# Bias tiles of one head loaded two heads ahead, value products one score group later, and a larger early part of the output projection, in a hybrid attention layer on one Trainium2 core

## The chip, the core and the metric

The kernel runs on one core of one Trainium2 chip. A core has five engines that work through queues of their own: TensorE (PE, matrix products), VectorE (DVE), ScalarE (ACT), GpSimd (POOL) and SyncE (SP), which here issues every DMA. They meet only at semaphores. The metric is the device time of one execution in microseconds (us); lower is better.

## What is computed

One layer of a hybrid decoder, for one sequence of 512 tokens and width 1024, with 256 memory tokens. The part that the change touches is the first block:

```python
h = rms_norm(x, norm_mix[l])
proj = h @ w_in[l]
qa, ka, va, qg, kg, vg, glr, rg = jnp.split(proj, offsets, axis=-1)
o_a = moba_attention(qa, ka, va, rp_table)      # 8 heads of 64, causal, with a bias by distance
o_g = gla_chunked(qg, kg, vg, log_a)            # 4 heads of gated linear attention
o_g = rms_norm(o_g, g_norm[l]).reshape(B, T, G_WIDTH) * jax.nn.silu(rg)
x = x + jnp.concatenate([o_a, o_g], axis=-1) @ w_out[l]
h = rms_norm(x, norm_xattn[l])
...
```

Cross attention into the memory tokens, a squared-ReLU MLP of width 4096 and a final norm follow; their code is the same before and after. With 512 tokens and blocks of 256 every past block is chosen, so the attention is plain causal attention with a bias that depends on the distance of query and key alone.

## The kernel before

**Numbers.** Each operand of a product is split into two fp16 parts, so one product of a 128-wide piece of the contraction is three matmuls (lines 227, 228, 229). One such piece, three matmuls, is called a step here. A generator yields after each step.

**Order.** The order on PE is written out by hand: `fill` is a queue of generators, and `fill(n)` takes n steps from it, between the pieces of the attention. The order on DVE, ACT, POOL and SP comes from a scheduler, and each of these works strictly through its own queue. The contraction of the output projection has eight pieces, `mix[0]` to `mix[7]`: `mix[p]` for p below 4 is the attention output of head pair p, and `mix[4]` to `mix[7]` are the gated linear attention heads, multiplied with their gate by `rg_steps`.

**Bias.** `bscr` in DRAM holds a bias table for each head. `Pair(p)` loads 128x256 of it for each of its two heads into one tile `bq` (two such tiles exist) and lets POOL spread column 256 over the left half.

**Attention.** The eight heads are taken as four pairs. For pair i and for g = 0 to 3, `score(3 - g)` makes the scores of 128 queries, of 512, 384, 256 and 128 keys, in two PSUM banks `s`. DVE adds the bias and takes the maximum (`p`, line 748), ACT takes the exponential (line 752), and after every second group the sums are inverted and ACT and DVE write the two fp16 parts of the probabilities (`pq`, lines 772 and 773). `trans()` sends the two heads' `pq` through two DMA transposes into `pT` (line 779). `attn_out(p)` multiplies `pT` with the values in 24 matmuls into a bank `o` (line 791), and ACT and DVE split it into `mix[p]` (lines 273 and 274). It is issued in the loop of the next pair, at g = 2. Between the groups `fill` brings the projections of pairs 2 and 3 (`qk`), then the four gates (`rg`).

**Output projection.** It is made in eight parts of 128 columns. For the first four, `early_steps` fills four PSUM banks with the pieces of `mix` that are there first, for all 512 tokens; `residual_steps` adds the rest, for each half of 256 tokens, adds the sum to `xr` (line 831) and collects squares for the norm. `ssq[hf].total()` sums them on PE, and `normed` makes `act2` of them, on which the next projection `xq` starts.

**Weights.** DMA brings them into five tiles `wst` of 512 KB; ACT and DVE turn each into two fp16 parts in one of ten tiles `whl` (lines 114 and 115). These conversions stand in the same queues.

Of the kernel before, what the change touches and what calls it, by code (L numbers as in the profile page):

```python
# [10 lines left out]
F32 = mybir.dt.float32  # L11
I32 = mybir.dt.int32
AF = mybir.ActivationFunctionType
ALU = mybir.AluOpType
AX = mybir.AxisListType

P = 128
T = 512
# [3 lines left out]
NEG = -1e30  # L22
# [16 lines left out]
def hybrid_block_kernel(  # L39
# [3 lines left out]
    nc = tc.nc  # L43
    PE, ACT, DVE, POOL = nc.tensor, nc.scalar, nc.vector, nc.gpsimd
# [16 lines left out]
    def gbank(name):  # L61
        return bank("pg", 3, name)

    def sbank(name):
        return bank("ps", 5, name)
# [155 lines left out]
    def gemm_steps(ps, key, act, c0=0, c1=T, kts=range(8), start=True, stop=True, base=0, **kw):  # L221
        wt = W.get(key).rearrange("p s (k c) -> p s k c", k=8)
        kts = list(kts)
        for i, kt in enumerate(kts):
            a = act[base + kt]
            st, sp = start and i == 0, stop and i == len(kts) - 1
            PE.matmul(ps, wt[:, 0, kt, :], a[:, 0, c0:c1], start=st, stop=False, **kw)  # L227
            PE.matmul(ps, wt[:, 0, kt, :], a[:, 1, c0:c1], start=False, stop=False, **kw)  # L228
            PE.matmul(ps, wt[:, 1, kt, :], a[:, 0, c0:c1], start=False, stop=sp, **kw)  # L229
            yield  # L230
# [39 lines left out]
    fill = Fill()  # L270
# [79 lines left out]
    mix = [m.bitcast(F16).rearrange("p (s t) -> p s t", s=2) for m in mixf]  # L350
    s1 = ExitStack()
    p1 = s1.enter_context(tc.tile_pool(name="p1", bufs=1))
# [46 lines left out]
    for n in range(8):  # L399
        ps = (sbank if n < 2 else gbank)(f"xk{n}")[:, :M]  # L400
# [28 lines left out]
    for c in range(2):  # L429
        for t in range(2):  # L430
            ps = gbank(f"xv{c}{t}")
# [21 lines left out]
    for i in range(2):  # L453
        for a, b in ((0, 0), (0, 1), (1, 0)):
            for j in range(4):
                kt = 2 * j + i
                PE.matmul(psg[32 * j:32 * j + 16, :], wg[:, a, kt, :], act1[kt][:, b, :],
                          start=(i == 0 and a == 0 and b == 0), stop=(i == 1 and a == 1),
# [220 lines left out]
    bscr = pdr.tile([8, P, T], F32, name="bscr")  # L679
# [3 lines left out]
        bass.AP(tensor=bscr1.tensor, offset=bscr1.offset, ap=[[NDIST, 8], [0, P], [1, NDIST]]),  # L683
    )

    gl = [Gla(0), Gla(1)]
    fill.add(gqk_steps(1), *[vg_steps(t) for t in range(4)])
    fill.add(*[va_steps(t) for t in range(4)], qk_steps(0), qk_steps(1))
    for pr in range(2):
        G = gl[pr]  # L690
        a = G.prep_fine()
        fill(20 if pr == 0 else 4)
        G.banks()
        G.small(0, a)
        for i, s in enumerate((8, 16)):
            a = G.prep_level(s)
            fill(2)
            G.small(128 + 128 * i, a)
        a = G.prep_level(32)
        fill(4)  # L700
        G.mid(a[0])
        a = G.prep_level(64)
        fill(4)
        G.large(a[0])
        G.prep_cross()
        fill(5)
        G.keys()
        fill(5)
        if pr == 0:
            fill.until(6)  # L710
        G.states()
        fill(4)
        G.outp()
        fill(6)
        for hh in range(2):
            G.norm(hh)
            fill(4)
# [5 lines left out]
    pt = s3.enter_context(tc.tile_pool(name="patt", bufs=1, reuse_waits="tile"))  # L723
# [3 lines left out]
    class Pair:  # L727
        def __init__(self, p):
            self.p, self.pr = p, {}
            bq = self.bq = pt.tile([P, 2, T], F32, tag="bq", bufs=2, name=f"bq{p}")  # L730
            for hh in range(2):
                nc.sync.dma_start(bq[:, hh, 256:], bscr[2 * p + hh, :, 127:383])
                POOL.tensor_copy(bq[:, hh, :256], bq[:, hh, 256:257].to_broadcast([P, 256]))
            self.sm = pt.tile([P, 3, 4, 2], F32, tag="sm4", bufs=2, name=f"sm4_{p}")

        def score(self, qt):
            p = self.p
            n = P * (qt + 1)
            pss = [sbank(f"s{p}_{qt}_{hh}")[:, :n] for hh in range(2)]
            qs = slice(qt * P, qt * P + P)  # L740
            for i, (a, b) in enumerate(((0, 0), (0, 1), (1, 0))):
                for hh, ps in enumerate(pss):
                    r = slice(64 * hh, 64 * hh + 64)
                    PE.matmul(ps, aq[p][r, a, qs], ak[p][r, b, :n], start=i == 0, stop=i == 2)
            mx, ng, sm = (self.sm[:, i, qt, :] for i in range(3))
            for hh, ps in enumerate(pss):
                s = self.pr[qt, hh] = pt.tile([P, n], F32, tag=f"p{qt}", bufs=2, name=f"p{p}_{qt}_{hh}")
                DVE.tensor_tensor_reduce(s, ps, self.bq[:, hh, T - n:], scale=1.0, scalar=NEG, op0=ALU.add, op1=ALU.max, accum_out=mx[:, hh:hh + 1])
            DVE.tensor_scalar(ng, mx, -1.0 / (SA * SA), None, op0=ALU.mult)
            for hh in range(2):  # L750
                s = self.pr[qt, hh]
                ACT.activation(s, s, AF.Exp, bias=ng[:, hh:hh + 1], scale=1.0 / (SA * SA), accum_out=sm[:, hh:hh + 1])
            if qt % 2 == 0:
                r = self.sm[:, 2, qt:qt + 2, :]
                DVE.reciprocal(r, r)
                DVE.tensor_scalar(r, r, SP, None, op0=ALU.mult)
                for q in (qt + 1, qt):
                    self.parts(q)
# [55 lines left out]
    early = {}  # L814

    def early_steps():
        for n in range(NPRE):
            early[n] = sbank(f"out{n}")
            yield from gemm_steps(early[n], ("out", n), mix, 0, T, (0, 1, 4, 5), stop=False, skip_group_check=True)

    def residual_steps(nm, act, hf, ssq):
        c0 = hf * HT
        for n in range(8):
            if nm == "out" and n < NPRE:
                ps = early[n][:, c0:c0 + HT]
                yield from gemm_steps(ps, (nm, n), act, c0, c0 + HT, (6, 7, 2, 3), start=False, skip_group_check=True)
            else:
                ps = gbank(f"{nm}{n}_{hf}")[:, :HT]
                yield from gemm_steps(ps, (nm, n), act, c0, c0 + HT)
            xs = xr[n][:, c0:c0 + HT]  # L830
            DVE.scalar_tensor_tensor(xs, ps, IS, xs, op0=ALU.mult, op1=ALU.add)
            ssq.add(xs)
# [8 lines left out]
    HT = T // 2  # L841
# [3 lines left out]
    for i in range(5):  # L845
        if i < 4:
            pairs[i] = Pair(i)
        if i in (2, 3):
            fill.until({2: 5, 3: 4}[i])
        if i == 4:  # L850
            fill.drain()
            load_xr()
            fill.add(early_steps(), residual_steps("out", mix, 0, ssq[0]))
        for g in range(4):
            if i < 4:
                pairs[i].score(3 - g)
                fill(2)
            if g > 0 and i >= 1:
                fill(2 if i < 4 else 4)
            if 1 <= i < 4 and g == 2:  # L860
                attn_out(pairs.pop(i - 1))
        if i < 4:
            pairs[i].trans()
            fill(2)
    fill(3)
    attn_out(pairs.pop(3))
    fill(1)
    s3.close()
    s1.close()

# [385 lines left out]
    for i, (a, b) in enumerate(parts[1:]):  # L1256
        ps = sbank(f"c3{i}")[:, :b - a]
# [100 lines left out]
```

## Time and profile before

| what | value |
|---|---|
| median of 3 runs | 724.23 us (721.04 to 724.78) |
| the profiled execution, its own time | 722.87 us |
| its span from first to last instruction | 721.1 us |
| PE busy | 686.4 us, 95% of the span |
| DVE busy | 551.3 us, 76% |
| ACT busy | 417.8 us, 58% |
| mean granted PE clock, as a share of full speed | 0.977 |

All times inside the execution are counted from the start of the span. A PE that is 95% busy leaves some 35 us in which it did nothing; where such a stretch lies, and whether what follows ran at full clock, is to be read from the timeline, stage by stage, since a mean over the span mixes stages with different limits.

### The profile page before, as it was taken

How to read it: one execution, taken by the hardware profiler on the slowest of the kernel's cores; microseconds unless marked ns; L12 is line 12 of the kernel's file. 1: busy time of each engine (PE TensorE's matmuls, PEld its weight loads, DVE VectorE, ACT ScalarE, POOL GpSimd, SP SyncE). 2: the span in 40 equal slices, each digit the busy share in tenths (PEclk: the TensorE clock that was granted, in tenths of full speed). 3: DMA queues.
4: the chain of work that ended last, by engine and by line, in shares of the span. 5: the costliest groups of instructions: out<-in, count | busy, mean ns of one | idle time of the engine just before them, and what ended most of it. 6: DMA issues, size and time to landing. Idle time of an engine off the chain costs nothing.

```text
span 721.1 us, 13438 instructions
## 1 busy us (share of the span) xinstructions
PE 686.4 (95%) x5370; PEld 472.7 (66%) x5370; DVE 551.3 (76%) x971; ACT 417.8 (58%) x803; POOL 81.7 (11%) x97
## 2 busy tenths in 40 slices
PE   6998999997889989999999999999999999999995
PEld 3843455453334478788888864458888866478884
DVE  7799772748858936947638899989887889999725
ACT  6686543545858816546536676565444766665633
POOL 4601000000000024200024200000000000003211
PEclk7999999999879999999999999999999999999998
DMA  8665722008366633316412423213333342314003
GB/s 315 225 237 183 257 88 89 2 30 262 71 153 147 202 101 118 117 41 165 129 20 77 157 78 99 72 46 119 117 117 117 119 149 86 116 39 143 26 1 118
DMA packets 56627, 85.62 MB, mean 119 GB/s; under 512 B 32075, under 2 KB 37492, under 8 KB 56564
## 3 DMA queue, kind: packets, MB, share of 16 engines
q1 hardware_dynamic: 56564, 84.76, 37.8%
q8 instruction: 42, 0.69, 0.4%
q14 instruction: 21, 0.17, 0.1%
HBM read 75.30 MB, written 3.68 MB: 110 GB/s over the span
## 4 chain that ended last, share of the span: by engine, by line
PE 55%; DVE 9%; ACT 3%; issue 2%; POOL 1%; DMA 1%; DVEq 0%; ACTq 0%; POOLq 0%
PE up L229 6%; PE up L227 6%; PE up L228 6%; PE a L1132 4%; PE a L1134 4%; PE a L1133 4%; DVE whl L115 2%; PE xq L229 2%; PE xq L228 2%; PE xq L227 2%; PE c L1132 2%; PE c L1133 2%; PE c L1134 2%; PE xo L229 1%; PE xo L228 1%
## 5 line engine op out<-in xcount | busy, mean ns | idle before, releaser
L115 DVE SCALAR_TENSOR_TENSOR whl<-wst,whl 128x1024 f16<-128x1024 f32 (+1 forms) x162 | 196.2, 1218 | 30.4 <-ACT whl L114 29.9
L114 ACT ACTIVATE whl<-wst 128x1024 f16<-128x1024 f32 (+1 forms) x162 | 165.6, 1029 | 32.4 <-PE a L1134 8.0
L229 PEld LDWEIGHTS <-whl 128*128 128x128 f16 x784 | 77.4, 99 | 48.3 <-issue 5.2
L227 PEld LDWEIGHTS <-whl 128*128 128x128 f16 x784 | 77.3, 99 | 46.1 <-issue 7.0
L228 PEld LDWEIGHTS <-whl 128*128 128x128 f16 x784 | 77.4, 99 | 39.3 <-issue 1.5
L227 PE MATMUL up<-act,whl 128*128 128x512 f16 (+1 forms) x224 | 78.1, 349 | 0.0
L228 PE MATMUL up<-act,whl 128*128 128x512 f16 (+1 forms) x224 | 78.1, 349 | 0.0
L229 PE MATMUL up<-act,whl 128*128 128x512 f16 (+1 forms) x224 | 78.1, 349 | 0.0
L1132 PE MATMUL a<-t,whl 128*128 128x256 f16 x192 | 52.3, 273 | 1.1 <-ACT v L1149 1.1
L1134 PE MATMUL a<-t,whl 128*128 128x256 f16 x192 | 52.3, 273 | 0.0
L1133 PE MATMUL a<-t,whl 128*128 128x256 f16 x192 | 52.3, 273 | 0.0
L1133 PEld LDWEIGHTS <-whl 128*128 128x128 f16 x456 | 44.6, 98 | 6.9 <-issue 1.5
L1132 PEld LDWEIGHTS <-whl 128*128 128x128 f16 x456 | 44.6, 98 | 5.2
L1134 PEld LDWEIGHTS <-whl 128*128 128x128 f16 x456 | 44.6, 98 | 5.0
L228 PE MATMUL xq<-act,whl 128*128 128x256 f16 x128 | 34.9, 273 | 0.2 <-DVE act L274 0.2
L229 PE MATMUL xo<-ox,whl 128*128 128x256 f16 x128 | 34.9, 273 | 0.0
L227 PE MATMUL xq<-act,whl 128*128 128x256 f16 x128 | 34.9, 273 | 0.0
L227 PE MATMUL xo<-ox,whl 128*128 128x256 f16 x128 | 34.9, 273 | 0.0
L228 PE MATMUL xo<-ox,whl 128*128 128x256 f16 x128 | 34.9, 273 | 0.0
L229 PE MATMUL xq<-act,whl 128*128 128x256 f16 x128 | 34.9, 273 | 0.0
L273 ACT ACTIVATE t<-hs 128x512 f16<-128x512 f32 x32 | 19.8, 624 | 23.9 <-DVE hs L1014 23.7
L227 PE MATMUL out<-mix,whl 128*128 128x256 f16 (+1 forms) x112 | 32.2, 288 | 0.0
(335 smaller groups left out, 1661.0 us busy)
## 6 DMA issues: line engine op xcount, KB each, us to landing
wst<-in_w_up SPq DMA_DIRECT2D x32, 512.0 KB, 3.7
wst<-in_w_down SPq DMA_DIRECT2D x32, 512.0 KB, 4.3
wst<-in_w_tt SPq DMA_DIRECT2D x16, 512.0 KB, 4.5
wst<-in_w_xv SPq DMA_DIRECT2D x8, 512.0 KB, 4.7
wst<-in_w_vv SPq DMA_DIRECT2D x8, 512.0 KB, 4.2
wst<-in_w_out SPq DMA_DIRECT2D x8, 512.0 KB, 4.7
wst<-in_w_xq SPq DMA_DIRECT2D x8, 512.0 KB, 3.8
wst<-in_w_xo SPq DMA_DIRECT2D x8, 512.0 KB, 4.4
```

Of the source, the lines that this page charges most:

```text
L114: ACT.activation(wt[:, 0, c], stg[:, c], AF.Copy, scale=SW)
L115: DVE.scalar_tensor_tensor(wt[:, 1, c], stg[:, c], SW, wt[:, 0, c], op0=ALU.mult, op1=ALU.subtract)
L227: PE.matmul(ps, wt[:, 0, kt, :], a[:, 0, c0:c1], start=st, stop=False, **kw)
L228: PE.matmul(ps, wt[:, 0, kt, :], a[:, 1, c0:c1], start=False, stop=False, **kw)
L229: PE.matmul(ps, wt[:, 1, kt, :], a[:, 0, c0:c1], start=False, stop=sp, **kw)
L273: ACT.activation(dst_h, src, AF.Copy, scale=scale)
L1132: PE.matmul(ps, w[:, 0, kt, :], b[:, 0, c], start=st, stop=False, skip_group_check=not start)
L1133: PE.matmul(ps, w[:, 0, kt, :], b[:, 1, c], start=False, stop=False, skip_group_check=not start)
L1134: PE.matmul(ps, w[:, 1, kt, :], b[:, 0, c], start=False, stop=sp, skip_group_check=not start)
```

## The change

Three edits. The bias tiles become tiles of one head. Four slots exist, three in a pool that is open throughout (`p1`), one in the attention's pool (`pt`), and `load_bias(p)` is called once before the second half of the gated linear attention, for pair 0, and then at the start of each pair for the next one. `attn_out(i - 1)` moves from g = 2 to g = 3, behind one more score group and its fill steps. And `early_steps` takes six of the eight pieces in place of four, in 24 steps instead of 16, all of them ahead of `attn_out(3)`.

```diff
+    bias = {}
+
+    def load_bias(p):
+        bias[p] = []
+        for hh in range(2):
+            h = 2 * p + hh
+            if h % 4 < 3:
+                bq = p1.tile([P, T], F32, tag="bq", bufs=3, name=f"bq{h}")
+            else:
+                bq = pt.tile([P, T], F32, tag="bq", bufs=1, name=f"bq{h}")
+            nc.sync.dma_start(bq[:, 256:], bscr[h, :, 127:383])
+            POOL.tensor_copy(bq[:, :256], bq[:, 256:257].to_broadcast([P, 256]))
+            bias[p].append(bq)
...
     for pr in range(2):
+        if pr == 1:
+            load_bias(0)
...
     class Pair:
         def __init__(self, p):
             self.p, self.pr = p, {}
-            bq = self.bq = pt.tile([P, 2, T], F32, tag="bq", bufs=2, name=f"bq{p}")
-            for hh in range(2):
-                nc.sync.dma_start(bq[:, hh, 256:], bscr[2 * p + hh, :, 127:383])
-                POOL.tensor_copy(bq[:, hh, :256], bq[:, hh, 256:257].to_broadcast([P, 256]))
+            self.bq = bias.pop(p)
...
-            yield from gemm_steps(early[n], ("out", n), mix, 0, T, (0, 1, 4, 5), stop=False, skip_group_check=True)
+            yield from gemm_steps(early[n], ("out", n), mix, 0, T, (0, 1, 4, 5, 6, 7), stop=False, skip_group_check=True)
...
-                yield from gemm_steps(ps, (nm, n), act, c0, c0 + HT, (6, 7, 2, 3), start=False, skip_group_check=True)
+                yield from gemm_steps(ps, (nm, n), act, c0, c0 + HT, (2, 3), start=False, skip_group_check=True)
...
             pairs[i] = Pair(i)
+            if i < 3:
+                load_bias(i + 1)
...
-            if 1 <= i < 4 and g == 2:
+            if 1 <= i < 4 and g == 3:
                 attn_out(pairs.pop(i - 1))
...
-    fill(3)
+    fill(12)
     attn_out(pairs.pop(3))
-    fill(1)
```

On SP, at the start of the attention, the bias loads of before stood behind six loads of output weights (`wst44` to `wst46` are the last of them; `bq0` and `bq1` are pairs here, `pT0` are pair 0's transposes).

```order
L113 DMA wst44_2613<-in_w_out 128x1024
L113 DMA wst45_2631<-in_w_out 128x1024
L113 DMA wst46_2649<-in_w_out 128x1024
L732 DMA bq0_1831<-bscr_832 128x256 x2
L732 DMA bq1_1972<-bscr_832 128x256 x2
L113 DMA wst47_2667<-in_w_out 128x1024
L732 DMA bq2_2161<-bscr_832 128x256 x2
L779 DMA_TRANSPOSE pT0_0_1953<-pq0_0_1881 128x20x128
L779 DMA_TRANSPOSE pT0_1_1955<-pq0_1_1882 128x20x128
```

In the changed kernel (`bq` is numbered by head) the first three loads stand in the gated linear attention, ahead of the last five loads of `w_tt`, and the fourth to sixth take the old place.

```order
L113 DMA wst35_1788<-in_w_tt 128x1024
L697 DMA bq0_1393<-bscr_832 128x256
L697 DMA bq1_1396<-bscr_832 128x256
L697 DMA bq2_1838<-bscr_832 128x256
L113 DMA wst36_1860<-in_w_tt 128x1024
...
L113 DMA wst46_2665<-in_w_out 128x1024
L697 DMA bq3_1841<-bscr_832 128x256
L697 DMA bq4_1980<-bscr_832 128x256
L697 DMA bq5_1983<-bscr_832 128x256
L113 DMA wst47_2689<-in_w_out 128x1024
L793 DMA_TRANSPOSE pT0_0_1960<-pq0_0_1888 128x20x128
L793 DMA_TRANSPOSE pT0_1_1962<-pq0_1_1889 128x20x128
```

The loads of heads 0, 1 and 2 moved far ahead; those of heads 4 and 5 now stand ahead of pair 0's transposes and reuse the slots of heads 0 and 1.

On PE, in the first of the four early banks (`out0` is the bank, `mix5` the second gated head), the next bank followed after `mix5`:

```order
L227 MATMUL out0_2612<-mix5_110,whl41_2349 128x512
L228 LDWEIGHTS whl41_2349
L228 MATMUL out0_2612<-mix5_110,whl41_2349 128x512
L229 LDWEIGHTS whl41_2349
L229 MATMUL out0_2612<-mix5_110,whl41_2349 128x512
L227 LDWEIGHTS whl42_2458
L227 MATMUL out1_2630<-mix0_105,whl42_2458 128x512
L228 LDWEIGHTS whl42_2458
```

Now `mix6` and `mix7` follow in the same bank, and every other early step stands behind them:

```order
L229 MATMUL out0_2616<-mix5_110,whl41_2358 128x512
L227 LDWEIGHTS whl41_2358
L227 MATMUL out0_2616<-mix6_111,whl41_2358 128x512
L228 LDWEIGHTS whl41_2358
L228 MATMUL out0_2616<-mix6_111,whl41_2358 128x512
L229 LDWEIGHTS whl41_2358
L229 MATMUL out0_2616<-mix6_111,whl41_2358 128x512
L227 LDWEIGHTS whl41_2358
L227 MATMUL out0_2616<-mix7_112,whl41_2358 128x512
```

So the first use of `mix6` is the fifth of now 24 early steps, and the first use of `mix7` the sixth; before, 15 of the 16 early steps stood ahead of `attn_out(3)`, and none of the 16 used `mix6` or `mix7`.

On DVE, the end of the attention before (`pq3` are the last probabilities of pair 3, `rge`, `rgu` and `rg` tiles of the gates of heads 2 and 3, which end in `mix6` and `mix7`):

```order
L773 SCALAR_TENSOR_TENSOR pq3_0_2403<-p3_0_0_2509,sm4_3_2364,pq3_0_2403 128x128
L773 SCALAR_TENSOR_TENSOR pq3_1_2404<-p3_0_1_2511,sm4_3_2364,pq3_1_2404 128x128
L809 SCALAR_TENSOR_TENSOR rge2_2542<-rg2_2456,rgu2_2543 128x512
L803 TENSOR_SCALAR rge3_2584<-rge3_2584 128x512
L810 TENSOR_TENSOR rge2_2542<-rge2_2542,mix6_111 128x512
L115 SCALAR_TENSOR_TENSOR whl50_2860<-wst50_2859,whl50_2860 128x1024
L274 SCALAR_TENSOR_TENSOR mix6_111<-rge2_2542,mix6_111 128x512
L807 SCALAR_TENSOR_TENSOR rge3_2584<-rge3_2584,rgu3_2585 128x512
L808 SCALAR_TENSOR_TENSOR rgu3_2585<-rge3_2584,rgu3_2585 128x512
L809 SCALAR_TENSOR_TENSOR rge3_2584<-rg3_2554,rgu3_2585 128x512
L810 TENSOR_TENSOR rge3_2584<-rge3_2584,mix7_112 128x512
L274 SCALAR_TENSOR_TENSOR mix7_112<-rge3_2584,mix7_112 128x512
```

The same in the changed kernel; the last write of `pq3` stands four rows ahead of the first row shown:

```order
L115 SCALAR_TENSOR_TENSOR whl49_2830<-wst49_2829,whl49_2830 128x1024
L822 SCALAR_TENSOR_TENSOR rgu2_2547<-rge2_2546,rgu2_2547 128x512
L817 TENSOR_SCALAR rge3_2588<-rge3_2588 128x512
L823 SCALAR_TENSOR_TENSOR rge2_2546<-rg2_2460,rgu2_2547 128x512
L115 SCALAR_TENSOR_TENSOR whl50_2864<-wst50_2863,whl50_2864 128x1024
L824 TENSOR_TENSOR rge2_2546<-rge2_2546,mix6_111 128x512
L821 SCALAR_TENSOR_TENSOR rge3_2588<-rge3_2588,rgu3_2589 128x512
L822 SCALAR_TENSOR_TENSOR rgu3_2589<-rge3_2588,rgu3_2589 128x512
L274 SCALAR_TENSOR_TENSOR mix6_111<-rge2_2546,mix6_111 128x512
L823 SCALAR_TENSOR_TENSOR rge3_2588<-rg3_2558,rgu3_2589 128x512
L824 TENSOR_TENSOR rge3_2588<-rge3_2588,mix7_112 128x512
L274 SCALAR_TENSOR_TENSOR mix7_112<-rge3_2588,mix7_112 128x512
```

Ten rows stood between the last write of `pq3` and `mix7`; now it is 15: `mix5`, `mix2`, the rest of gate 2, two weight conversions and gate 3 come behind `pq3`.

## Rows read from the trace of the kernel before

**Rows 1.** The page, busy time by engine: us, share of the span, instructions.

```profile
PE 686.4 (95%) x5370; PEld 472.7 (66%) x5370; DVE 551.3 (76%) x971; ACT 417.8 (58%) x803; POOL 81.7 (11%) x97
```

**Rows 2.** Waits of PE, 160 to 300 us: total us, times, longest.

```profile
PE o L791 <- DMA pT<-pq: 8.6, 4, 3.3
```

**Rows 3.** Windows: busy us of PE, weight loads, DVE, ACT, POOL; PE clock, DMA.

```profile
140.00:160.00 20.00, 20.00 (x191) 11.09 (x188) 10.31 (x25) 8.39 (x20) 0.00 (x0) 1.00 0.01 2
...
179.60:183.00 3.40, 3.40 (x15) 1.06 (x16) 2.34 (x12) 2.25 (x7) 0.29 (x1) 0.52 0.03 12
...
201.30:206.70 5.40, 5.40 (x34) 3.15 (x34) 1.28 (x6) 0.88 (x2) 0.00 (x0) 0.50 0.31 125
254.40:256.60 2.20, 0.09 (x3) 0.02 (x2) 0.69 (x1) 0.41 (x1) 0.00 (x0) 1.00 1.03 192
...
226.95:255.53 28.58, 27.44 (x152) 12.30 (x150) 26.76 (x63) 21.15 (x46) 0.00 (x0) 1.00 0.82 199
...
276.97:293.50 16.53, 16.42 (x149) 14.48 (x148) 15.99 (x30) 13.60 (x26) 8.44 (x7) 1.00 0.38 128
```

**Rows 4.** Timeline of DVE: start, us, instruction, [idle before it and its releaser].

```profile
172.43 0.75 DVE L662 SCALAR_TENSOR_TENSOR mix<-go,gneg,wg 128x512 f32<-128x512 f32 x1
...
176.08 0.75 DVE L662 SCALAR_TENSOR_TENSOR mix<-go,gneg,wg 128x512 f32<-128x512 f32 x1
178.84 0.69 DVE L748 CUSTOM_DVE_ANT_0 p<-s,bq 128x512 f32<-128x512 f32 x1 [2.02 <-POOL bq L733]
```

**Rows 5.** Timeline of PE, 176 to 205 us.

```profile
176.88 0.28 PE L744 MATMUL s<-qks,qks 64*128 64x256 f16 x1 [1.40 <-DVE mix L662]
179.59 0.70 PE L744 MATMUL s<-qks,qks 64*128 64x256 f16 x5 [2.43 <-DVE sm L748]
...
191.84 0.39 PE L227 MATMUL qk<-act,whl 128*128 128x512 f16 x1
...
194.23 0.38 PE L229 MATMUL qk<-act,whl 128*128 128x512 f16 x1
197.35 0.63 PE L791 MATMUL o<-pT,vas 128*64 128x512 f16 x1 [2.74 <-DMA pT<-pq]
201.25 3.36 PE L791 MATMUL o<-pT,vas 128*64 128x512 f16 x23 [3.27 <-DMA pT<-pq]
```

**Rows 6.** SP's first transposes, all transposes' time to landing, and the bias copies.

```profile
192.16 6.34 SPq L779 DMA_TRANSPOSE pT<-pq  x2
...
DMA to landing us min/median/max: 4.9/5.1/6.5
...
L733 POOL COPY bq<-bq x8: 396/426/653, 178.4 to 209.4; 128x256 f32<-128x256 f32 x8
```

**Rows 7.** Timeline of DVE: the last probabilities of each pair, and mix7.

```profile
190.96 1.40 DVE L773 SCALAR_TENSOR_TENSOR pq<-p,sm,pq 128x256 f16<-128x256 f32 x4
...
208.35 1.68 DVE L773 SCALAR_TENSOR_TENSOR pq<-p,sm,pq 128x256 f16<-128x256 f32 x4 [0.64 <-ACT pq L772]
...
225.15 1.41 DVE L773 SCALAR_TENSOR_TENSOR pq<-p,sm,pq 128x256 f16<-128x256 f32 x4 [0.64 <-ACT pq L772]
...
247.09 1.00 DVE L773 SCALAR_TENSOR_TENSOR pq<-p,sm,pq 128x256 f16<-128x256 f32 x3
...
254.84 0.69 DVE L274 SCALAR_TENSOR_TENSOR mix<-rge,mix 128x512 f16<-128x512 f32 x1 [0.69 <-ACT mix L273]
```

**Rows 8.** Timeline of PE and DVE: the last value products, and their split.

```profile
256.57 1.79 PE L791 MATMUL o<-pT,vas 128*64 128x512 f16 x23 [2.11 <-DMA pT<-pq]
...
259.03 0.69 DVE L274 SCALAR_TENSOR_TENSOR mix<-o,mix 128x512 f16<-128x512 f32 x1 [3.50 <-ACT mix L273]
```

**Rows 9.** Timeline of PE and DVE: the norm behind the output projection.

```profile
276.97 0.60 PE L327 MATMUL ssqout<-accout,ones 128*128 128x256 f32 x2
...
293.10 0.41 DVE L274 SCALAR_TENSOR_TENSOR act<-ynout,act 128x256 f16<-128x256 f32 x1
...
296.95 0.70 PE L327 MATMUL ssqout<-accout,ones 128*128 128x256 f32 x2 [1.37 <-POOL accout L322]
```

More of the change, by code (lines that the diff above doesn't have):

```diff
@@ L747, in score @@
                 s = self.pr[qt, hh] = pt.tile([P, n], F32, tag=f"p{qt}", bufs=2, name=f"p{p}_{qt}_{hh}")
-                DVE.tensor_tensor_reduce(s, ps, self.bq[:, hh, T - n:], scale=1.0, scalar=NEG, op0=ALU.add, op1=ALU.max, accum_out=mx[:, hh:hh + 1])
+                DVE.tensor_tensor_reduce(s, ps, self.bq[hh][:, T - n:], scale=1.0, scalar=NEG, op0=ALU.add, op1=ALU.max, accum_out=mx[:, hh:hh + 1])
             DVE.tensor_scalar(ng, mx, -1.0 / (SA * SA), None, op0=ALU.mult)
```

## Prediction

> **What bounds the kernel now.** I read the page first: PE is busy for 686.4 of the 721.1 us of the span [rows 1], so it is the bound nearly everywhere, and a change of order can gain only where PE stands still. The sum of PE's waits in the stretch that the change touches names the largest: 8.6 us in four waits of the value products for the DMA transposes [rows 2]. The timeline then shows the places. PE stops before the scores of 256 keys of pair 0, 1.40 and then 2.43 us [rows 5]; the second wait ends when DVE has read the first scores, and DVE itself had stood still for 2.02 us until POOL had spread the bias [rows 4]. At `attn_out(0)` PE waits 2.74 and 3.27 us for the two transposes [rows 5], and at `attn_out(3)` 2.11 us [rows 8]. The windows show what follows a wait: after the first place the granted clock is 0.52 for 3.4 us, after the second 0.50 for 5.4 us, which is the 1.2 GHz level; around the 2.11 us it stays at 1.00 [rows 3]. The second thing to see is DVE. From the first maximum of pair 3 to `mix7` it is busy for 26.76 of 28.58 us [rows 3]: the end of the attention is DVE's, not PE's.
>
> **The change, step by step.** I follow the new queues with the durations of before. A step is 12 matmuls in four, so from 191.84 to 194.23 with 11 spacings 0.217 us a matmul, 0.65 us a step [rows 5].
>
> *Bias.* The loads of heads 0 to 2 now go out some 75 us before they are read, so the wait of DVE for POOL goes. What is late next is DVE's own queue: from 172.43 to 176.08 [rows 4] it runs five instructions (a `mix`, a weight conversion, three short ones), the new order has the same five ahead of the first maximum, and that starts at 176.1 instead of 178.84. The second `mix`, which frees a score bank, now stands behind it and ends near 177.4; PE then goes on at 177.4 instead of 179.6, after a wait of about 2.1 us, and I take no fall of clock there (the 2.11 us wait had none, the 2.43 us wait did). The copies on POOL are as many as before; three of them, at most 0.65 us each [rows 6], move to about 136 us, where they could hold DVE for 0 to 2 us, but PE is never idle there, 20.00 of 20 us busy [rows 3], so I take 0. The six bias loads ahead of pair 0's transposes on SP end when pair 0's scores are read, at about 180.4, long before the transposes can start; 0 to 0.5 us, and I take 0.
>
> *Pair 0 to the transposes.* DVE ended pair 0's probabilities at 190.96 + 1.33 = 192.3, 13.4 us after the first maximum [rows 4, 7]. The new order puts one `mix` (0.65) and one conversion (1.14) in between, and takes away waits for scores of about 2.2; I get 13.0 us, the end at 189.1.
>
> *Value products one group later.* Between the old and the new place of `attn_out(0)` lie one score group (0.3) and four steps (2.6). From 177.4 PE has 20 steps (13.0) and six score groups (2.9) to go and arrives at 193.3. The second transpose landed at 201.25, 9.1 us after the first was issued [rows 5, 6]; 189.1 + 9.1 = 198.2. So the wait doesn't go: it is 4.9 us in place of 6.0, because pair 0 moved PE forward too. After such a wait the clock was at 0.50 [rows 3], so the products take 3.36 us again (1.79 at full clock, as the last ones do [rows 5, 8]; bounds 0 and 1.6 us for the fall): the end is 201.5 instead of 204.6.
>
> *The chain to mix7.* ACT stands behind these products in its queue, so pair 1 can't pass them: a split, a conversion and the last probabilities need 4.1 us, the end of pair 1 is 205.6 (before 208.35 + 1.66 = 210.0 [rows 7]). Pair 2 took 16.5 us from there to 226.5, with 3.5 us of waits of DVE; its scores are now long ready and I take 2.1 us off: 220.0. From there to `mix7` it was 29.0 us, to 255.5 [rows 7]. DVE is the limit, and its new queue holds one conversion (1.14) less: 28.1 us. So `mix7` is there at 248.1 and, 2.6 us of queue earlier, `mix6` at 245.5. That is 7.4 us earlier than before.
>
> *More early steps.* From 201.5 PE has 44 steps to the first use of `mix6` (28.6), eight score groups (4.1), two products (4.4) and 0.6 of low clock: it arrives at 239.2. There is nothing else it could issue, since 19 steps stand behind in its queue. **A new wait** of 6.3 us for `mix6`, one step, 1.9 us for `mix7`. Then two matmuls and 18 steps (12.1), the last products without a wait (2.2), and the price of the clock: between 0 and 2.8 us (what 5.4 us at half clock cost, less its floor: 1.57 in the products and 1.2 in the steps [rows 3, 5]); I take the middle, 1.4. End of the last products: 248.1 + 12.1 + 2.2 + 1.4 = 263.8, against 256.57 + 1.79 = 258.4 [rows 8]: **5.4 us later**.
>
> *What the rest is spared.* Behind these products stood one step and 96 short ones of 0.327 us; now there are 80. To the first sum of squares it was 276.97 − 258.4 = 18.6 us [rows 9]; now 16.3, with 0.9 us for the split of `mix[3]`, which two other pieces used to cover and which ended 1.3 us after the products [rows 8]. From there to the second sum it was 20.0 us [rows 9]. PE has 2.6 us less to do in it, but `act2` is DVE's again, which is busy for 15.99 of the 16.53 us up to its last write [rows 3, 9]; the new queue holds one conversion more, and that write is some 17 us after the sum. Only the 1.37 us wait for POOL [rows 9] goes: 18.9 us. Spared: 2.3 + 1.1 = **3.4 us**.
>
> **The sum:** + 5.4 − 3.4 = + 2.0 us on the profiled execution's 722.87. That execution lies 1.4 us below the median of the three runs; on 724.23 the forecast is 726.2 us.
>
> *A rule against a row.* The two transposes take 9.1 us together, each moving 128 x 20 x 128 fp16 values, 0.66 MB, with a median landing of 5.1 us [rows 6], or 128 GB/s. The Trainium skill, page "DMA: Bandwidth & Descriptors", section "Latency and other measured facts", gives a DMA transpose an effective 261 GB/s, by which both would be through in 5.0 us, an estimate from that page. By it `attn_out(0)` would hardly wait and the sum would be about 722.6 on the median. The measurement decides; I keep 9.1 us.
>
> **Rivals.** Half a per cent, 3.6 us, is about what a measurement of this kernel can tell from no change.
>
> *Forecast (chance 0.55):* a chain on DVE that starts earlier, and a new wait of PE that eats it. + 2.0 us; its own range is 722 to 729.
>
> *Slower: the clock (0.25).* After the new wait the fall costs the full 2.8, and it falls a second time: with 2.6 us less cover, `xq` waits about 3 us for the last `act2`, where it waited under 0.2. If more than about 2.4 us of that come in one piece (the shortest wait behind which the clock fell [rows 3, 5]), 1.6 to 2.8 us are lost. For it: both kinds of wait have rows at 0.50. Against it: the waits for `act2` come in pieces, and 2.11 us left the clock alone. + 5 to + 6 us: 729 to 731.
>
> *Faster: `mix6` and `mix7` are there in time (0.14).* Each us by which DVE's chain ends earlier than 248.1 is a us of the total, until PE arrives at 239.2; then the new wait and its clock are gone, worth 8.2 + 1.4: − 7.4 us, 717. It decides from `mix7` at 242.5, which is − 3.6; I price it at the middle, 719. For it: DVE had waits of 3.5 us in pair 2 and 1.8 in pair 3, of which I gave back only part. Against it: 15 instructions stand between pair 3's probabilities and `mix7`, and the windows leave DVE little idle.
>
> *The transposes land early (0.06):* by whatever cause `attn_out(0)` doesn't wait. Pair 1 then ends at 202.0, where its own exponentials limit it, 3.6 us earlier: 722.6, no change. Against it stand all eight transposes of before.
>
> **Numbers.** Slower by over 0.5%: the clock's 0.25 and 0.02 of the forecast's upper end. Faster: 0.14 and 0.02 of the transposes' case (with the clock kept). Within: 0.57. The range reaches from 720, which leaves out most of the faster case, to 731.5, the upper end of the slower one.
>
> **What would show it.** The first maximum at 176, not behind POOL: right for the bias. `attn_out(0)` still waiting 4 to 5 us for `pT`: right for the transposes; under 1 us: wrong. `mix7`'s split ending near 248 and PE idle some 8 us before it, in the first early bank: right for the new wait; `mix7` before 243, or PE later than 243 at that place, makes the prediction wrong. Granted clock 0.5 behind that wait for less than 2 or more than 5 us moves the sum by 1.4 either way. `xq` waiting 3 us for `act2`, and no wait at the second sum, show the part that is spared; if `xq` doesn't wait, the gain there is 2.6 us larger.

## The result and the profile after

The changed kernel takes 732.01 us (median, 730.45 to 732.87), the kernel before 724.01 us; the ratio is 1.0116 with a 95% interval of 1.0082 to 1.0150. It is slower by 1.2%, 5.8 us above the forecast of 726.2 and just outside its range. The profiled execution took 732.59 us with a span of 730.8, so the two profiles that are compared here lie 9.7 us apart, the medians 8.0.

The sum of TensorE's waits in the stretch of the change (what waited, on what, total us, times, longest) answers to [rows 2]:

```profile
PE out L227 <- ACT mix L273: 6.9, 3, 5.7
PE o L805 <- DMA pT<-pq: 3.8, 2, 3.6
PE xq L228 <- DVE act L274: 3.0, 4, 1.0
PE s L758 <- DVE sm L762: 1.3, 1, 1.3
PE out L228 <- DVE mix L274: 1.1, 2, 0.7
PE xq L227 <- ACT act L273: 0.5, 1, 0.5
```

The waits for the transposes fell from 8.6 to 3.8 us and those at the first scores from 3.8 to 1.7. In their place stand 8.0 us in the output projection (7.3 of them for `mix6` and `mix7`, the rest later for `mix3`), and 3.5 us for `act2` ahead of the cross attention, where there were 0.2. The timeline of PE shows the places:

```profile
199.72 3.36 PE L805 MATMUL o<-pT,vas 128*64 128x512 f16 x23 [3.58 <-DMA pT<-pq]
...
247.08 0.58 PE L227 MATMUL out<-mix,whl 128*128 128x512 f16 x1 [5.66 <-ACT mix L273]
248.34 0.59 PE L228 MATMUL out<-mix,whl 128*128 128x512 f16 x1 [0.68 <-DVE mix L274]
250.33 0.58 PE L227 MATMUL out<-mix,whl 128*128 128x512 f16 x1 [0.98 <-ACT mix L273]
...
264.76 1.82 PE L805 MATMUL o<-pT,vas 128*64 128x512 f16 x24
...
294.37 0.27 PE L227 MATMUL xq<-act,whl 128*128 128x256 f16 x1
295.53 0.27 PE L228 MATMUL xq<-act,whl 128*128 128x256 f16 x1 [0.89 <-DVE act L274]
...
298.52 0.37 PE L228 MATMUL xq<-act,whl 128*128 128x256 f16 x1 [0.88 <-DVE act L274]
...
301.78 0.37 PE L228 MATMUL xq<-act,whl 128*128 128x256 f16 x1 [1.05 <-DVE act L274]
```

The windows of the changed kernel (as in [rows 3]: busy us of PE, weight loads, DVE, ACT, POOL; then granted clock and DMA):

```profile
60.00:73.00 13.00, 9.74 (x45) 3.29 (x45) 12.53 (x15) 9.66 (x13) 0.00 (x0) 0.74 0.70 233
177.80:181.00 3.20, 2.06 (x12) 0.71 (x11) 3.20 (x12) 0.65 (x2) 0.34 (x1) 1.00 0.57 189
199.72:203.08 3.36, 3.36 (x24) 2.42 (x24) 0.47 (x2) 0.00 (x0) 0.80 (x2) 0.52 0.79 297
247.08:254.30 7.22, 5.42 (x12) 1.63 (x12) 3.20 (x5) 0.63 (x1) 0.00 (x0) 0.51 0.95 305
266.55:282.97 16.42, 15.68 (x143) 13.77 (x142) 5.12 (x12) 5.09 (x12) 5.94 (x8) 1.00 0.01 1
294.37:305.70 11.33, 7.87 (x41) 4.99 (x39) 10.39 (x20) 5.70 (x12) 5.16 (x3) 0.70 0.35 114
300.00:305.00 5.00, 3.95 (x19) 2.45 (x18) 4.74 (x7) 1.09 (x3) 3.79 (x1) 0.50 0.33 111
```

and two of the kernel before, the first the same stretch, the second the same work as the line from 294.37 us above:

```profile
60.00:73.00 13.00, 9.51 (x51) 3.55 (x51) 12.37 (x15) 10.45 (x15) 0.00 (x0) 0.87 0.70 227
290.83:296.95 6.12, 4.58 (x41) 3.71 (x38) 6.12 (x10) 3.01 (x6) 4.53 (x2) 1.00 0.34 106
```

Two things are to be seen. The line from 294.37 us and the last line hold the same work, the steps of `xq` up to the second sum of squares: 6.12 us before, of which 4.58 are work and 1.54 waits, and 11.33 after, of which 7.87 are work and 3.47 waits. The 3.3 us more of work are the low clock. What the low clock costs the kernel is less, as the experiments show, since part of it lies where TensorE would else have waited longer. And the first lines show a difference that is not the change's: the instructions of TensorE are the same in both kernels there, but the clock was low for longer. The first matmul of `gk` starts at 71.83 us before and at 73.16 after; over the profiles of all kernels of this study it lies anywhere from 70.33 to 74.15. The changed kernel's profile was 1.3 us late before the change began, which leaves 8.4 of the 9.7 us. Another 0.45 us is the change's: from there to the first scores it is 99.44 us before and 99.89 after; in the kernels with the bias edit it is 99.76 to 99.92, in those without 99.44 to 99.61. The prediction had taken 0 for the copies on POOL there, between 0 and 2. In the points below these 1.8 us are taken off each time of the changed kernel's profile.

The timeline of DVE, the rows that answer to [rows 4] and [rows 7]:

```profile
177.80 0.68 DVE L762 CUSTOM_DVE_ANT_0 p<-s,bq 128x512 f32<-128x512 f32 x1
...
189.37 1.41 DVE L787 SCALAR_TENSOR_TENSOR pq<-p,sm,pq 128x256 f16<-128x256 f32 x4
...
205.83 1.40 DVE L787 SCALAR_TENSOR_TENSOR pq<-p,sm,pq 128x256 f16<-128x256 f32 x4
...
221.35 1.40 DVE L787 SCALAR_TENSOR_TENSOR pq<-p,sm,pq 128x256 f16<-128x256 f32 x4
...
247.61 0.68 DVE L274 SCALAR_TENSOR_TENSOR mix<-rge,mix 128x512 f16<-128x512 f32 x1
...
250.31 0.69 DVE L274 SCALAR_TENSOR_TENSOR mix<-rge,mix 128x512 f16<-128x512 f32 x1 [0.69 <-ACT mix L273]
```

The chain on VectorE does start and end earlier than before, `mix7` by 4.5 us in spite of the late start of the profile; and still TensorE is there first.

### The profile page after: what moved, and what is told of

It is laid out like the page before. It is cut to its first block, busy times and chain, and to the rows that moved or that the text cites. A ratio compares the mean times of both kernels' runs of the same rounds, so it can differ in the third digit from the quotient of the medians.

```text
span 730.8 us, 13395 instructions
## 1 busy us (share of the span) xinstructions
PE 691.7 (95%) x5346; PEld 471.3 (64%) x5346; DVE 549.9 (75%) x971; ACT 416.4 (57%) x803; POOL 81.4 (11%) x97
## 4 chain that ended last, share of the span: by engine, by line
PE 55%; DVE 8%; ACT 2%; issue 1%; POOL 1%; DMA 1%; DVEq 0%; ACTq 0%; POOLq 0%
PE up L228 6%; PE up L229 6%; PE up L227 6%; PE a L1147 4%; PE a L1149 4%; PE a L1148 4%; DVE whl L115 2%; PE xq L228 2%; PE xq L229 2%; PE xq L227 2%; PE c L1148 2%; PE c L1149 2%; PE c L1147 2%; PE out L228 1%; PE out L229 1%
## 5 line engine op out<-in xcount | busy, mean ns | idle before, releaser
L228 PE MATMUL xq<-act,whl 128*128 128x256 f16 x128 | 36.1, 282 | 3.0 <-DVE act L274 3.0
L227 PE MATMUL xq<-act,whl 128*128 128x256 f16 x128 | 36.0, 281 | 0.5 <-ACT act L273 0.5
L229 PE MATMUL xq<-act,whl 128*128 128x256 f16 x128 | 36.2, 283 | 0.0
```

## Experiments

Times are medians in us, ratios are to the kernel before on the same chip, with their 95% interval.

| kernel | time | ratio |
|---|---|---|
| changed kernel | 732.0 | 1.0116 (1.0082 to 1.0150) |
| e1: early steps piece by piece | 721.0 | 0.9962 (0.9950 to 0.9975) |
| e2: without the third edit | 714.5 | 0.9873 (0.9853 to 0.9893) |
| e3: third edit for half the tokens | 716.5 | 0.9896 (0.9880 to 0.9912) |
| e4: third edit alone | 737.1 | 1.0179 (1.0162 to 1.0196) |
| e5: bias edit alone | 721.6 | 0.9959 (0.9943 to 0.9975) |
| e6: later value products alone | 716.4 | 0.9886 (0.9864 to 0.9907) |
| e7: e1 and dead work ahead of `xq` | 720.2 | 0.9942 (0.9922 to 0.9962) |
| e8: e2 and three more steps | 712.3 | 0.9832 (0.9811 to 0.9853) |
| e9: of e6 only the steps | 726.4 | 1.0033 (1.0013 to 1.0052) |
| e10: of e6 only the scores | 718.6 | 0.9932 (0.9905 to 0.9959) |
| e11: e6 and three more steps | 714.8 | 0.9875 (0.9852 to 0.9897) |

**What does the third edit cost, and by what?** Theory A was the prediction's: `mix6` and `mix7` stand too far ahead in TensorE's queue, and the cover of `act2` is shorter. Theory B: VectorE sets the end whatever TensorE does.

e1 only reorders the early steps:

```diff
-            yield from gemm_steps(early[n], ("out", n), mix, 0, T, (0, 1, 4, 5, 6, 7), stop=False, ...)
+            yield from gemm_steps(early[n], ("out", n), mix, 0, T, (0, 1, 4, 5), stop=False, ...)
+        for kt in (6, 7):
+            for n in range(NPRE):
+                yield from gemm_steps(early[n], ("out", n), mix, 0, T, (kt,), start=False, stop=False, ...)
```

> The changed kernel with one alteration: the 24 early steps go over the four banks with pieces 0, 1, 4, 5 first, then piece 6 of all four banks, then piece 7. Theory A (order): TensorE waits for mix6 and mix7 only because they stand fifth and sixth. The first use of mix6 moves 12 steps (7.8 us) back, from 241.4 to about 249.2, when mix6 is there (248.3); so the 8.0 us of waits and some 1.9 us of low clock behind them go, and the time is 722, 10 us under the changed kernel; the waits for act2 (3.5 us) and the low clock there stay. Theory B (VectorE): the end of the attention is VectorE's, the wait only moves to the last value products or to the output projection behind them, and the time is 728 or more.

721.0 measured. The waits of TensorE in its profile behind pair 3 (what waited, on what, total us, times, longest):

```profile
PE xq L228 <- DVE act L274: 2.9, 4, 1.0
PE xq L227 <- ACT act L273: 0.5, 1, 0.5
PE out L228 <- DVE mix L274: 0.5, 1, 0.5
PE out L227 <- ACT mix L273: 0.3, 1, 0.3
```

The waits for the gates are gone (the two `out` rows are for `mix3`), those for `act2` unchanged. The order of 24 steps was worth 11 us. But this is only 3 us under the kernel before, with two edits in it that should give more.

e2 undoes the third edit: `(0, 1, 4, 5)` early, `(6, 7, 2, 3)` behind, `fill(3)` and `fill(1)` as before.

> The changed kernel with the third edit undone: 16 early steps of four pieces, 15 of them ahead of the last value products. Theory A: the third edit alone cost the time. The last value products end near 252, some 14.5 us earlier than in the changed kernel; the sum of squares comes 2.2 us more behind them, the waits for act2 (3.5 us), the low clock there (about 3 us) and the wait for xpT (0.8) go: 716, 8 us below the kernel before. Theory B: VectorE's queue, not the early steps, sets the end; mix6 and mix7 at 248 to 251 still hold the output projection and the first two edits gain under 3 us: 721 to 725.

714.5, 1.5 us under theory A; the profile has 0.2 us of waits at `xq` and none for the gates. The third edit thus costs 17.5 us on top of the other two. Done by half, with pieces 6 and 7 early only for the first 256 tokens (e3), it costs the second half no cover:

```diff
+        for kt in (6, 7):
+            for n in range(NPRE):
+                yield from gemm_steps(early[n][:, :HT], ("out", n), mix, 0, HT, (kt,), start=False, stop=False, ...)
...
-                yield from gemm_steps(ps, (nm, n), act, c0, c0 + HT, (2, 3), start=False, ...)
+                yield from gemm_steps(ps, (nm, n), act, c0, c0 + HT, (2, 3) if hf == 0 else (6, 7, 2, 3), ...)
```

> The first two edits kept; early steps with pieces 0, 1, 4, 5 of all four banks for all tokens, and then pieces 6 and 7 for the first 256 tokens alone (8 short steps, 2.6 us), so that the second half keeps its four pieces as cover for act2. Theory A: no wait over 1 us at the last value products, none of note for act2, full clock throughout: 715 to 716, the same as without the third edit or up to 1 us below it. Theory B: as without the third edit, 721 to 725.

716.5, as theory A had it to half a us, but no gain: e2 has nothing left to cover at the last value products (no wait there), and e3 waits 1.2 us for `mix7` and `mix3` instead.

e4 is the third edit on the kernel before:

> The kernel before with the third edit alone (six pieces, 24 early steps in bank order). Theory A: TensorE reaches mix6 at 246.9 and waits until it is split at 251.4, then for mix7 until 255.5; the last value products end near 271 instead of 258.4, the rest is spared 2.2 us and pays 3 to 4 us at act2: 735 to 738, slower than the changed kernel, since the first two edits help it. Theory B: the first two edits are what costs (copies on GpSimd in the linear attention, later value products), and the third alone gives 722 to 726.

737.1. On its own it costs 12.8 us, and with the first two edits 17.5. Two differences make most of the 4.7 us: the waits for `mix6` and `mix7` are 6.2 us in e4 and 7.3 in the changed kernel, and the wait of 2.1 us at the last value products, which the longer early part covers in e4, isn't there to be covered in e2. In e4 too the clock is low around the wait, 0.50 from 250 to 256 us and 0.67 from 256 to 262.

**Is it the clock at `xq`?** e7 is e1 with 22 dead matmuls ahead of `xq`:

```diff
     def xq_steps(hf):
+        if hf == 0:
+            wt = W.get(("xq", 0))
+            psd = gbank("cover")
+            for _ in range(22):
+                PE.matmul(psd, wt[:, 0, 0:P], wt[:, 0, 0:T], start=True, stop=True)
```

> The changed kernel with the early steps piece by piece over the four banks (721.0), and 22 matmuls of 512 columns into a bank that nobody reads (4.8 us at full clock), ahead of the projection xq of the first half, where TensorE waits 3.4 us in five pieces for act2 and its clock then stands at 0.50 for some 6 us. Theory A: the thin work there brings the low clock and that costs about 3 us beside the waits: with the dead work the waits go, the clock stays at 1.00, and the time falls to 718.5 to 719.5 although TensorE has 4.8 us more to do. Theory B: the low clock there has another cause, or costs nothing since act2 or the sum of squares is the limit: 721 to 723.

720.2, between the two theories; the stage itself decides. From the first to the second sum of squares, e1:

```profile
271.94:283.34 11.40, 11.40 (x103) 9.98 (x102) 9.09 (x14) 7.83 (x16) 5.84 (x6) 1.00 0.57 184
283.34:294.98 11.64, 8.29 (x41) 5.24 (x39) 10.40 (x20) 5.70 (x12) 5.17 (x3) 0.63 0.38 128
```

and e7, the middle line being the dead work:

```profile
273.65:284.89 11.24, 11.24 (x103) 9.97 (x102) 8.92 (x14) 7.67 (x15) 5.67 (x6) 1.00 0.55 181
284.89:289.64 4.75, 4.75 (x25) 2.16 (x22) 4.75 (x12) 3.79 (x9) 1.52 (x2) 1.00 0.41 127
289.64:295.67 6.03, 4.59 (x40) 3.71 (x38) 5.73 (x10) 2.09 (x5) 4.94 (x1) 1.00 0.35 101
```

The clock is at 1.00 throughout, so it is the thin stretch that brings the low clock. 23.04 us against 22.02 with 4.75 us of work added says that the low clock costs some 1.0 us here; the medians are 0.8 us apart, but their runs overlap (720.96 to 722.00 and 719.53 to 721.74). It is not worth the whole 3.3 us, since e7 still waits, 0.6 us for `act2` and 0.8 for POOL's sum: the norm's chain is the limit. The same stretch cut at the last write of `act2`, first the changed kernel, then e7:

```profile
282.97:302.06 19.09, 15.63 (x124) 12.41 (x123) 16.77 (x31) 13.15 (x26) 9.28 (x8) 0.91 0.44 138
302.06:305.70 3.64, 3.64 (x21) 2.56 (x19) 2.70 (x4) 0.38 (x1) 1.73 (x1) 0.55 0.63 207
...
273.65:292.77 19.12, 18.51 (x147) 14.25 (x146) 16.80 (x31) 13.16 (x26) 9.29 (x8) 1.00 0.43 138
292.77:295.67 2.90, 2.06 (x19) 1.59 (x17) 2.60 (x3) 0.39 (x1) 2.85 (x1) 1.00 0.73 210
```

The last write of `act2` ends 19.1 us behind the first sum in both, whatever the clock. Before it was 16.5 [rows 3, 9], and it is 16.5 in e2 and 16.6 in e3, in which the second half keeps its four pieces. The whole stretch between the two sums is 20.0 us in each kernel in which it does (before, e2, e3, e5, e6 and e8 to e11), and 22.0 to 23.0 in those in which it doesn't (the changed kernel, e1, e4, e7), although TensorE has less to do there. The changed kernel's timeline of ACT and DVE shows where its chain is held up:

```profile
286.42 0.42 ACT L311 ACTIVATE sqout<-xr 128x256 f32<-128x256 f32 x1 [1.54 <-POOL accout L322]
...
288.12 1.23 DVE L115 SCALAR_TENSOR_TENSOR whl<-wst,whl 128x1024 f16<-128x1024 f32 x1 [2.32 <-ACT whl L114]
```

With two pieces left per bank, sums of the second half come every 0.65 us (1.3 before), faster than POOL adds up their squares (1.57 us to start, then 3.20 for three). ScalarE's next square waits 1.54 us until POOL has read one of the two tiles for squares, and a step of the norm (line 281, which starts 3.8 us behind the sum in place of 2.3) and its half of a weight conversion stand behind it in its queue; VectorE then waits 2.32 us for that half. This is read from the trace; no run changes it alone.

**What are the other two edits worth?** e5 is the bias edit alone.

> The kernel before with the first edit alone (bias tiles of one head, loaded early; value products at their old place, 16 early steps). Both edits together took 9.8 us off. Theory A: the bias is the larger part: the first maximum no longer waits for GpSimd, the waits of TensorE at the scores of pair 0 fall from 3.8 to 1.7 us and the low clock of 3.4 us behind them (1.7 us lost) goes, and with it all that follows starts some 3 to 4 us earlier, also the transposes: 720 to 721. Some 0.4 us are paid near 137 us, where the copies on GpSimd now lie. Theory B: the value products take the gain back, since TensorE waits 6 us for the transposes in any case: 722.5 to 724.

721.6, a ratio of 0.9959 or 3.0 us, between the theories and nearer to A: the waits at the scores are 1.7 us and the clock behind them is 1.00, but the waits for the transposes grow to 9.4.

e6 is the later value products alone (g = 3 instead of 2).

> The kernel before with the second edit alone (each pair's value products behind one more score group and its fill steps). Theory A: the work of 2.9 us that is moved ahead of the first value products fills half of TensorE's 6.0 us there, the second wait of 3.3 us and the low clock behind it stay, and all four waits of the value products are 5 to 6 us in place of 8.6: 720 to 721.5. Theory B: the transposes end when VectorE's chain lets them, what is moved ahead is missing as cover at the last value products, whose wait grows from 2.1 to 5 us: 723.5 to 725.

Both theories fell: 716.4, 8.1 us off. The wait at the last value products neither stayed nor grew; it is gone. (Up to 1.8 us of its profile's gain lie elsewhere: TensorE's wait for the first maximum is 0.67 us in place of 2.43, since the bias landed sooner behind its issue in that run, at most 3.5 us against 5.4. Whether the runs without a profile had this too isn't known.) The edit moves two things ahead of the products, so they were tried apart. e9 moves only the four fill steps (and leaves them out at g = 3), e10 only the score group (the products stand at g = 3, the steps behind them):

```diff
 e9:
             if 1 <= i < 4 and g == 2:
+                fill(4)
                 attn_out(pairs.pop(i - 1))
 e10:
                 pairs[i].score(3 - g)
+                if 1 <= i and g == 3:
+                    attn_out(pairs.pop(i - 1))
                 fill(2)
```

> The second edit (8.1 us by itself) split in two. Here the kernel before with only the four fill steps (2.6 us) moved ahead of each pair's value products; the last score group (128 keys) stays behind them. Theory A (cover): what counts is work of TensorE under the wait for the transposes; the steps are 2.6 of the 2.9 us moved, the waits of 8.6 us fall by 3 to 5 us, and most of the gain is here: 718 to 720. Theory B (queues): what counts is that the last scores stand ahead of the value products, whose split in the queues of ScalarE and VectorE no longer holds up the last exponentials and probabilities of the pair; then the steps alone give 722.5 to 724, and the last value products wait longer.

> The other half of the second edit: the last score group (0.3 us) moved ahead of the value products, the four fill steps left behind them. Theory A (cover): nearly nothing is moved under the wait, 723 to 724. Theory B (queues): the probabilities of pairs 1, 2 and 3 come 2 to 7 us earlier, the wait of 2.1 us at the last value products goes, and most of the 8.1 us is here: 717 to 719.

726.4 and 718.6: theory B. By the ratios, moving 2.6 us of work under the wait costs 2.4 us (e9 waits 11.1 us for the transposes in place of 8.6, as pair 2's probabilities end at 229.4 instead of 226.5), and moving 0.3 us of scores gives 4.9. The timeline of ScalarE at `attn_out(0)` shows why. Before (start, us, instruction, idle before it and its releaser):

```profile
204.65 0.60 ACT L273 ACTIVATE mix<-o 128x512 f16<-128x512 f32 x1 [4.36 <-PE o L791]
206.42 0.40 ACT L752 ACTIVATE p<-p,sm 128x128 f32<-128x128 f32 x1 [1.18 <-DVE sm L749]
...
207.81 1.49 ACT L772 ACTIVATE pq<-p,sm 128x256 f16<-128x256 f32 x4 [0.51 <-DVE sm L756]
```

e9:

```profile
205.27 0.60 ACT L273 ACTIVATE mix<-o 128x512 f16<-128x512 f32 x1 [2.87 <-PE o L791]
206.77 0.40 ACT L752 ACTIVATE p<-p,sm 128x128 f32<-128x128 f32 x1 [0.90 <-DVE sm L749]
...
208.71 1.49 ACT L772 ACTIVATE pq<-p,sm 128x256 f16<-128x256 f32 x4 [1.06 <-DVE sm L756]
```

e10:

```profile
202.35 0.60 ACT L273 ACTIVATE mix<-o 128x512 f16<-128x512 f32 x1 [3.52 <-PE o L791]
202.85 1.48 ACT L772 ACTIVATE pq<-p,sm 128x256 f16<-128x256 f32 x4
```

Before and in e9 the last exponentials of pair 1 (128 keys) come behind the split, since their scores stand behind the value products; the probabilities start 3.2 and 3.4 us behind the split's start. In e10 the exponentials ran while TensorE waited, and the probabilities follow after 0.5 us. With the later pairs the distance shrinks too, from 3.3 to 1.9 us in pair 2 (where the exponentials still come behind the split) and from 6.7 to 2.9 in pair 3, and the scheduler puts more of the gate work behind `pq3`: pair 3's probabilities end at 248.1 us before, 248.7 in e9, and 242.0 in e10 and in e6 (each in its own profile; e10's began 1.5 us early, e6's 1.4 us late).

The two halves don't add up: 4.9 us gained and 2.4 lost are 2.5, and e6, which has both, gains 8.1. So once the scores have passed, the same four steps are worth 3.2 us (the intervals of e6 and e10 just touch). Here cover paid only behind the scores.

e8 takes up where e2 waits longest, 3.5 us at the first value products with the clock low behind it, and e11 does the same without the bias edit:

```diff
+            if i == 1 and g == 3:
+                fill(3)
             if 1 <= i < 4 and g == 3:
                 attn_out(pairs.pop(i - 1))
```

> The first two edits, without the third (714.5), and three more fill steps (1.95 us) ahead of the first value products, taken from the last pairs' fill. Theory A: the wait of 3.5 us at the first value products shrinks to 1.6 us, behind which the clock does not fall, so these products take 1.8 in place of 3.2 us, and the 2 us of work done early come back as a wait of about 2 us at the last value products, without a fall: 712.5 to 713.5. Theory B: the clock falls at the last value products instead, or VectorE's chain to the last gates takes the gain: 714 to 715.5.

> The second edit alone and three more fill steps ahead of the first value products, that is the fastest kernel so far (712.3) without the bias edit. Theory A: the bias edit still gives the 2 us that it gave beside the second edit (716.4 to 714.5): 714 to 715. Theory B: with the value products' wait split, the first maximum no longer matters, since the transposes of pair 0 have cover enough: 712 to 713.

712.3 and 714.8, theory A for both, e8 a little under its range. Against e2 the three steps gain 2 to 3 us (their intervals just touch); e11 can't be told from e6, as their intervals overlap. The two waits of e8's value products, first and last pair:

```profile
199.53 1.79 PE L805 MATMUL o<-pT,vas 128*64 128x512 f16 x23 [1.98 <-DMA pT<-pq]
...
246.64 1.79 PE L805 MATMUL o<-pT,vas 128*64 128x512 f16 x23 [1.26 <-DMA pT<-pq]
```

One wait of 3.5 us became two of 1.98 and 1.26, the products run in 1.79 us at full clock, and the kernel is the fastest of all, 1.7% under the kernel before.

## Why the prediction was wrong

Times of the changed kernel's profile less 1.8 us, as said above, beside the prediction's.

| step | predicted | measured |
|---|---|---|
| first maximum | 176.1 | 176.0 |
| pair 0's probabilities end | 189.1 | 188.9 |
| `attn_out(0)` ends | 201.5 | 201.3 |
| pairs 1 and 2 end | 205.6, 220.0 | 205.4, 220.9 |
| `mix6`, `mix7` split | 245.5, 248.1 | 246.5, 249.2 |
| TensorE reaches `mix6` | 239.2 | 239.6 |
| waits for `mix6` and `mix7` | 6.3 + 1.9 | 6.3 + 1.0 |
| low clock behind them | 1.4 (0 to 2.8) | 2.1 |
| last value products end | 263.8 | 264.8 |
| from there to the first sum of squares | 16.3 | 16.4 |
| from there to the last write of `act2` | some 17 | 19.1 |
| from the first sum to the second | 18.9 | 22.7 |
| behind it | 0 | + 0.9 |

*Bias, pair 0, value products, chain to `mix7`, new wait:* right, each within about 1 us. `attn_out(0)` still waits, 3.6 us (4.9 were said) for the second transpose: from the first issue at 190.58 to the products at 199.72 it is 9.1 us again. The Trainium skill (page "DMA: Bandwidth & Descriptors", section "Latency and other measured facts") gives a DMA transpose an effective rate; by an estimate from it `attn_out(0)` would hardly have waited. This trace does not agree. The low clock was 2.1 us: 57 matmuls from 250.33 to 264.76 took 14.4 us, at 0.217 us each they are 12.4. It lies inside its bounds. `mix7` was 1.1 us late, all of it in pair 2, off whose 16.5 us I had taken 2.1 where it was 1.0 (15.5 from 207.15 to 222.66). (Between the last write of `pq3` and `mix7` stand 14 rows, and 9 before: 15 and 10 count `mix7` itself. The difference is the same.) These two make the last value products 1.0 us later than predicted: 6.4 us behind the kernel before, where 5.4 was said.

*What the rest is spared:* here the prediction failed, in the term "From there to the second sum": that the last write of `act2` "is some 17 us after the sum" and that, as only the wait for POOL goes, the stretch is 18.9 us. It was 22.7. The prediction took VectorE as busy all the way and let its queue alone set the write; but the two pieces that the third edit takes out of each bank let the squares pile up on POOL, ScalarE waits for POOL, VectorE waits 2.32 us for ScalarE, and the write ends at 19.1 us, also in e7, where the clock stays at 1.00. (The sum was too small by its own prices: 16.5 us before and one conversion of 1.14 more are 17.7.) That is 2.1 us of the 3.8. The other 1.7 are the clock: it was at 0.50 behind the waits for `act2`, and what TensorE has to do behind the write took 3.6 us in place of the 1.9 that the sum left for it. At full clock it would not all come back, since POOL's sum is then late; e7 gives 1.0 of it. The waits for `act2` came as forecast in size (3.5 us for "about 3"), but by luck: with the chain as late as that and a full clock they would have been longer.

The rival "Slower: the clock", with a chance of 0.25, had the fall at `xq`, and what was held against it was wrong: "the waits for `act2` come in pieces, and 2.11 us left the clock alone". So was its condition, a piece of over 2.4 us: the longest is 1.05 us, and the window of 300 to 305 us shows 0.50. It did not have the longer chain, so that it came near the measured time is in part luck. Its price of 729 to 731 was short as well, since the cross attention then waited 0.8 us for its first transposes, where it had not, and the last products were late by 1.0.

The sum, measured: 6.4 − 2.2 + 2.7 + 0.9, and 0.45 for the copies, is 8.2 us, against 8.0 between the medians. Of the 6.2 us between this sum and the forecast's 2.0, 3.8 are the stretch between the two sums of squares (2.1 the chain to `act2`, 1.7 the clock behind it), 1.0 the last value products, 0.9 the wait behind and 0.45 the copies. The upper end of the range was the rival's own upper end, without the spread of the other terms on it: that is why 732.0 lies outside.

*The gain side* came out in its times and not in its cause. The prediction credited the later value products with 0.3 + 2.6 us of cover. By itself such cover costs 2.4 us (e9) and pays only together with the scores; what counts first is that the last scores pass the value products in the queues of ScalarE and VectorE (e10), a thing that the prediction used only in the other direction ("ACT stands behind these products in its queue").

What stays open: the scheduler's reordering of VectorE's queue came with e6, e9 and e10 and was not tried by itself, so what it gives and what the passing of the split gives are not told apart; the squares that pile up on POOL were not slowed or spread by themselves; and why the first matmul of `gk` starts at a different time from profile to profile.

## What to carry to other kernels

Where an engine works strictly through a queue, an early start for a sum is worth its place: put the terms whose operands come last at the end of the whole batch, over all accumulators, not at the end of each (11 us here for the same 24 steps). Work that is taken from behind a norm is not simply saved; before moving it, add up the norm's chain on all the other engines, with the waits between them and at the new pace of the sums that feed it (here the stretch grew from 20.0 us to between 22 and 23, with less to do on TensorE), and price the clock for the thin stretch as a whole, not by the longest single wait. And when a consumer must wait for a transfer, look first at what stands behind it in the queues of the other engines: 0.3 us of scores passed ahead gave 4.9 us, and 2.6 us of cover gained only behind them.

## What was not expected of the hardware

How long the last wait was does not say whether the clock falls. At `xq` of the changed kernel it was at 0.50 behind pieces of at most 1.05 us. In e9, waits of 2.60 and 2.78 us left it at 1.00, while 2.61 and 3.52 us earlier in the same run did not. The windows of e9 that begin with the instruction behind these four waits (2.61, 3.52, 2.60 and 2.78 us):

```profile
180.24:183.50 3.26, 3.26 (x18) 1.21 (x18) 2.39 (x13) 2.11 (x7) 0.24 (x1) 0.63 0.01 5
201.96:206.00 4.04, 4.04 (x32) 2.82 (x32) 0.68 (x6) 1.04 (x2) 0.00 (x0) 0.62 0.41 162
237.36:241.00 3.64, 3.64 (x37) 2.33 (x37) 2.90 (x5) 3.64 (x7) 0.00 (x0) 1.00 0.02 5
258.21:262.00 3.79, 3.79 (x39) 2.93 (x39) 0.69 (x1) 0.60 (x1) 0.00 (x0) 1.00 0.29 116
```

And behind a stretch that no edit touches, the first matmul of `gk` starts anywhere from 70.33 to 74.15 us, which moves the rest by up to 3.8 us, as much as half of this change. The clock from 60 to 73 us was 0.74 in some of these profiles and 0.87 in others, but that alone doesn't order them: e1 starts at 72.59 with 0.87, e4 at 72.46 with 0.74.
